# Binary cross-entropy over 8192 x 8192: three prediction slots and one 8-bit target slot in place of two slots each

## The chip, the cores and the metric

The kernel runs on one core of a Trainium2 chip. The metric is the device time of one execution in microseconds; the median of several runs is given. The work of this kernel is done by four kinds of unit: VectorE (DVE in the profile), ScalarE (ACT), GpSimd (POOL), which here only issues transfers, and the core's 16 DMA engines, which move data between HBM and SBUF. SyncE (SP) issues a few transfers too.

## The reference

```python
def setup_inputs():
    return {
        "pred": np.random.uniform(0.01, 0.99, (8192, 8192)).astype(np.float32),
        "target": np.random.randint(0, 2, (8192, 8192)).astype(np.float32),
    }

def reference(pred, target):
    eps = 1e-7
    pred = np.clip(pred, eps, 1 - eps)
    return -(target * np.log(pred) + (1 - target) * np.log(1 - pred))
```

Both inputs and the output are 8192 x 8192 in float32, 268.4 MB each. A target is 0 or 1. The kernel uses that: with p the clipped prediction and t the target, p + t - 1 is p where t is 1 and p - 1 where t is 0, so the natural logarithm of its absolute value, negated, is the result in both cases.

## The kernel before, in words

The matrices are read as flat arrays and cut into chunks. A chunk of width w is 128 partitions of w contiguous elements; the whole array is 524,288 columns of this kind. The function `plan` sets the widths and places: two chunks of 7680 columns, then 32 of 15360, two of 7680 and one of 1696; a side piece of 32 partitions x 1408 elements holds the remainder. SBUF has a ring of two slots of 15360 columns (60 KiB a partition) for predictions in float32 and one of the same columns for targets in bf16, with a small place for the last chunk. Targets are converted on the way in: the DMA reads float32 and writes bf16. The results overwrite the predictions in place and are stored from there.

Each chunk has five passes, most in two halves of 7680 columns:

- clip, L92, on DVE;
- merge, L95, on DVE (`scalar_tensor_tensor`: t - 1 + p);
- absolute value, L98, and logarithm, L99, on ACT;
- negate, L102, on DVE.

The order is written out by hand (`tc.manual_schedule()`): each engine does its instructions in the order of the program and waits at each for what it needs. Almost all transfers are issued by POOL into one queue, and the DMA engines serve that queue in order. In the main loop a chunk k is clipped and merged half by half, then negated half by half; then POOL gets the store of k (L78), the load of the targets of k+2 (L73) and the load of the predictions of k+2 (L74). With two slots, the last of these has to wait until the store of k has landed, since it writes into the same slot; POOL waits there with everything behind it. The first prediction chunk, the side piece and the last three stores go through SP's queue.

Of the kernel before, what the change touches and what calls it, by code (L numbers as in the profile page):

```python
# [1 line left out]

# [4 lines left out]

EPS = 1e-7

BIG = 15 * 1024  # L10
HALF = BIG // 2
SIDE = 1408


def plan(total):

    n, last = divmod(total, BIG)
    assert n > 4 and 0 < last <= 2048
    spots = [(HALF, 0), (HALF, HALF)]
    spots += [(BIG, k % 2 * BIG) for k in range(1, n - 1)]  # L20
    end = (n - 1) % 2 * BIG
    return spots + [(HALF, end), (HALF, end + HALF), (last - SIDE // 4, 2 * BIG)]

@with_exitstack
def kernel(
    ctx: ExitStack,
    tc: tile.TileContext,
    pred: bass.AP,  # L30
    target: bass.AP,
    out: bass.AP,
):
    nc = tc.nc
    fp32 = mybir.dt.float32
    bf16 = mybir.dt.bfloat16
    Alu = mybir.AluOpType
    Act = mybir.ActivationFunctionType
    P = nc.NUM_PARTITIONS

    R, C = pred.shape
    spots = plan(R * C // P)
    n = len(spots)
    widths = [w for w, _ in spots]
    turn = n // 2
    cut = R * C - sum(widths[:turn]) * P
    starts = [cut + sum(widths[:k]) * P for k in range(turn)]
    starts += [sum(widths[turn:k]) * P for k in range(turn, n)]

    def chunk(ap, k):  # L50
        flat = ap.rearrange("r c -> (r c)")
        return flat[starts[k] : starts[k] + widths[k] * P].rearrange("(p w) -> p w", p=P)

    pool = ctx.enter_context(tc.tile_pool(name="rings", bufs=1))
    ring = [P, 2 * BIG + widths[-1]]
    ring_p = pool.tile(ring, fp32, name="ring_p", tag="ring_p")
    ring_t = pool.tile(ring, bf16, name="ring_t", tag="ring_t")
    warm = pool.tile([1, 8], fp32, name="warm", tag="warm")
    side_p = pool.tile([32, SIDE], fp32, name="side_p", tag="side_p")
    side_t = pool.tile([32, SIDE], fp32, name="side_t", tag="side_t")  # L60

    def side(ap, j):
        flat = ap.rearrange("r c -> (r c)")
        return flat[cut - 32 * SIDE : cut].rearrange("(p w) -> p w", p=32)[j:32:4]

    def spot(ring, k, part=(0, 1)):
        w, c = spots[k]
        i, m = part
        return ring[:, c + i * w // m : c + (i + 1) * w // m]

    def load(k):
        queue = nc.sync if k == 0 else nc.gpsimd
        nc.gpsimd.dma_start(out=spot(ring_t, k), in_=chunk(target, k))  # L73
        queue.dma_start(out=spot(ring_p, k), in_=chunk(pred, k))  # L74

    def store(k):
        queue = nc.sync if k >= n - 3 else nc.gpsimd
        queue.dma_start(out=chunk(out, k), in_=spot(ring_p, k))  # L78

    def load_side():  # L80
        nc.vector.memset(side_p[:, 0:2], 0.5)  # L81
        nc.vector.memset(side_t[:, 0:2], 0.0)  # L82
        for j in range(4):
            nc.sync.dma_start(out=side_t[j:32:4, :], in_=side(target, j))
            nc.sync.dma_start(out=side_p[j:32:4, :], in_=side(pred, j))

    def store_side():
        for j in range(4):
            nc.sync.dma_start(out=side(out, j), in_=side_p[j:32:4, :])

    def front_of(p, t):
        nc.vector.tensor_scalar(  # L92
            out=p, in0=p, scalar1=EPS, scalar2=1 - EPS, op0=Alu.max, op1=Alu.min
        )
        nc.vector.scalar_tensor_tensor(  # L95
            out=p, in0=t, scalar=1.0, in1=p, op0=Alu.subtract, op1=Alu.add
        )
        nc.scalar.activation(out=p, in_=p, func=Act.Abs)  # L98
        nc.scalar.activation(out=p, in_=p, func=Act.Ln)  # L99

    def back_of(p):
        nc.vector.tensor_scalar(out=p, in0=p, scalar1=-1.0, scalar2=None, op0=Alu.mult)  # L102

    def front(k, *part):
        front_of(spot(ring_p, k, *part), spot(ring_t, k, *part))

    def back(k, *part):
        back_of(spot(ring_p, k, *part))

    with tc.manual_schedule():  # L110
        nc.vector.memset(warm, 1.0)  # L111
        for k in range(3):
            load(k)
        nc.scalar.activation(out=warm, in_=warm, func=Act.Ln)  # L114
        front(0)
        front(1)
        back(0)
        store(0)
        back(1)
        store(1)  # L120
        load(3)
        for k in range(2, n - 4):
            front(k, (0, 2))
            front(k, (1, 2))
            back(k, (0, 2))
            back(k, (1, 2))
            store(k)
            if k == n - 6:
                load_side()
            if k == n - 5:  # L130
                front_of(side_p, side_t)
            for j in range(k + 2, n if k == n - 5 else k + 3):
                load(j)
        z, a, b, c = range(n - 4, n)
        front(z, (0, 2))
        back_of(side_p)
        store_side()
        front(z, (1, 2))
        back(z, (0, 2))
        front(a)  # L140
        back(z, (1, 2))
        store(z)
        front(b, (0, 2))
        front(b, (1, 2))
        back(a)
        store(a)
        front(c)
        back(b)
        store(b)
        back(c)  # L150
        store(c)


# [1 line left out]
_INS = ['pred', 'target']  # L155
_OUTS = [((8192, 8192), 'float32')]


# [23 lines left out]
```

## Time and profile before

| quantity | value |
|---|---|
| time, median of 3 runs | 1865.92 us (1865.59 to 1866.86) |
| the profiled execution: its span | 1864.3 us |
| DVE busy | 1124.7 us (60%) |
| ACT busy | 902.1 us (48%) |
| POOL busy | 57.6 us (3%) |
| DMA, moved as counted in SBUF | 671.22 MB, mean 360 GB/s |
| HBM read and written | 536.87 MB and 268.44 MB, 432 GB/s |

The profiled execution has no timing of its own beside its span; the span runs from the first to the last instruction, and the median of the timed runs is 1.6 us longer. Lines of the timeline read: start in us, length in us, engine, line of the kernel, operation, output<-input, shapes, and in brackets the idle time of the engine just before and what ended it. Lines of the stretches read: from:to, length, busy time of DVE, ACT and POOL with the number of instructions, granted clock, mean busy share of the 16 DMA engines, GB/s. A packet counts wholly in the stretch in which it starts, so that in very short stretches the share can be above 1. Behind the views lie the trace's packet records (start, length and size of each DMA packet); here a packet of a large transfer is one partition's row.

### The profile page before, as it was taken

How to read it: one execution, taken by the hardware profiler on the slowest of the kernel's cores; microseconds unless marked ns; L12 is line 12 of the kernel's file. 1: busy time of each engine (PE TensorE's matmuls, PEld its weight loads, DVE VectorE, ACT ScalarE, POOL GpSimd, SP SyncE). 2: the span in 40 equal slices, each digit the busy share in tenths (PEclk: the TensorE clock that was granted, in tenths of full speed). 3: DMA queues.
4: the chain of work that ended last, by engine and by line, in shares of the span. 5: the costliest groups of instructions: out<-in, count | busy, mean ns of one | idle time of the engine just before them, and what ended most of it. 6: DMA issues, size and time to landing. Idle time of an engine off the chain costs nothing.

```text
span 1864.3 us, 649 instructions
## 1 busy us (share of the span) xinstructions
DVE 1124.7 (60%) x215; ACT 902.1 (48%) x144; POOL 57.6 (3%) x111
## 2 busy tenths in 40 slices
DVE  4655766555676655557665555766555576655585
ACT  3355553335555333555533355553335555333665
POOL 0000000000000000000000000000000000000000
DMA  9999999999999999999999999999999999999999
GB/s 295 376 357 340 357 339 370 386 380 355 341 355 343 369 388 379 356 341 355 349 364 388 380 355 343 353 353 360 389 378 355 349 348 353 359 388 384 347 341 385
DMA packets 16180, 671.22 MB, mean 360 GB/s; under 512 B 1872, under 2 KB 1872, under 8 KB 2352
## 3 DMA queue, kind: packets, MB, share of 16 engines
q0 software_dynamic: 15408, 657.98, 98.4%
q1 hardware_dynamic: 768, 13.21, 1.7%
q14 instruction: 4, 0.03, 0.0%
HBM read 536.87 MB, written 268.44 MB: 432 GB/s over the span
## 4 chain that ended last, share of the span: by engine, by line
DMA 35%; issue 26%; ACT 22%; DVE 15%; POOL 1%; DVEq 0%; POOLq 0%; PEldq 0%
DMA ring_p<-in_pred_dram 32%; ACT ring_p L98 11%; ACT ring_p L99 11%; DVE ring_p L95 7%; DVE ring_p L92 4%; DVE ring_p L102 4%; DMA out_dram<-ring_p 3%; POOL ring_t L73 0%; POOL out_dram L78 0%; DVEq L177 0%; POOL ring_p L74 0%; POOLq L78 0%; POOLq L73 0%; DVEq L92 0%; PEldq L177 0%
## 5 line engine op out<-in xcount | busy, mean ns | idle before, releaser
L98 ACT ACTIVATE ring_p<-ring_p 128x7680 f32<-128x7680 f32 (+1 forms) x70 | 450.3, 6433 | 933.4 <-DVE ring_p L95 933.4
L95 DVE SCALAR_TENSOR_TENSOR ring_p<-ring_t,ring_p 128x7680 f32<-128x7680 bf16 (+1 forms) x70 | 556.9, 7955 | 2.4
L92 DVE TENSOR_SCALAR ring_p<-ring_p 128x7680 f32<-128x7680 f32 (+1 forms) x70 | 283.8, 4055 | 397.9 <-DMA ring_p<-in_pred_dram 397.9
L102 DVE TENSOR_SCALAR ring_p<-ring_p 128x7680 f32<-128x7680 f32 (+1 forms) x69 | 283.8, 4114 | 321.2 <-ACT ring_p L99 321.2
L99 ACT ACTIVATE ring_p<-ring_p 128x7680 f32<-128x7680 f32 (+1 forms) x70 | 450.8, 6440 | 2.2
L74 POOL DMA_DIRECT2D ring_p<-in_pred_dram x36 | 19.3, 536 | 909.5 <-DMA out_dram<-ring_p 909.5
L78 POOL DMA_DIRECT2D out_dram<-ring_p x34 | 18.3, 539 | 852.0 <-DVE ring_p L102 827.7
L73 POOL DMA_DIRECT2D ring_t<-in_target_dram x37 | 20.3, 550 | 0.8 <-PEq L177 0.8
L98 ACT ACTIVATE side_p<-side_p 32x1408 f32<-32x1408 f32 x1 | 1.4, 1375 | 6.7 <-DVE side_p L95 6.7
L114 ACT ACT_TABLE_LOAD x1 | 1.3, 1283 | 0.7 <-PEq L166 0.7
L95 DVE SCALAR_TENSOR_TENSOR side_p<-side_t,side_p 32x1408 f32<-32x1408 f32 x1 | 1.6, 1611 | 0.0
L99 ACT ACTIVATE side_p<-side_p 32x1408 f32<-32x1408 f32 x1 | 1.4, 1375 | 0.0
L92 DVE TENSOR_SCALAR side_p<-side_p 32x1408 f32<-32x1408 f32 x1 | 0.9, 874 | 0.0
L102 DVE TENSOR_SCALAR side_p<-side_p 32x1408 f32<-32x1408 f32 x1 | 0.9, 873 | 0.0
L111 DVE MEMSET warm<- 1x8 f32 x1 | 0.1, 65 | 0.8 <-PEq L166 0.8
L114 ACT ACTIVATE warm<-warm 1x8 f32<-1x8 f32 x1 | 0.2, 208 | 0.0
L166 POOL MEMSET const-float32-0.0<- 128x1 f32 x1 | 0.1, 98 | 0.2 <-issue 0.2
L166 POOL MEMSET const-bfloat16-1.0<- 128x1 bf16 x1 | 0.1, 101 | 0.0
L166 POOL MEMSET const-uint8-127<- 128x1 uint8 x1 | 0.1, 99 | 0.0
L166 POOL MEMSET const-float32-1.0<- 128x1 f32 x1 | 0.1, 98 | 0.0
L81 DVE MEMSET side_p<- 32x2 f32 x1 | 0.1, 60 | 0.0
L82 DVE MEMSET side_t<- 32x2 f32 x1 | 0.1, 60 | 0.0
## 6 DMA issues: line engine op xcount, KB each, us to landing
ring_p<-in_pred_dram POOLq DMA_DIRECT2D x32, 7680.0 KB, 35.9
out_dram<-ring_p POOLq DMA_DIRECT2D x32, 7680.0 KB, 29.2
ring_t<-in_target_dram POOLq DMA_DIRECT2D x32, 3840.0 KB, 46.8
ring_p<-in_pred_dram POOLq DMA_DIRECT2D x3, 3840.0 KB, 35.7
ring_t<-in_target_dram POOLq DMA_DIRECT2D x4, 1920.0 KB, 28.2
out_dram<-ring_p POOLq DMA_DIRECT2D x2, 3840.0 KB, 28.1
out_dram<-ring_p SPq DMA_DIRECT2D x2, 3840.0 KB
ring_p<-in_pred_dram SPq DMA_DIRECT2D x1, 3840.0 KB
```

Of the source, the lines that this page charges most:

```text
L73: nc.gpsimd.dma_start(out=spot(ring_t, k), in_=chunk(target, k))
L74: queue.dma_start(out=spot(ring_p, k), in_=chunk(pred, k))
L78: queue.dma_start(out=chunk(out, k), in_=spot(ring_p, k))
L81: nc.vector.memset(side_p[:, 0:2], 0.5)
L82: nc.vector.memset(side_t[:, 0:2], 0.0)
L92: nc.vector.tensor_scalar(out=p, in0=p, scalar1=EPS, scalar2=1 - EPS, op0=Alu.max, op1=Alu.min)
L95: nc.vector.scalar_tensor_tensor(out=p, in0=t, scalar=1.0, in1=p, op0=Alu.subtract, op1=Alu.add)
L98: nc.scalar.activation(out=p, in_=p, func=Act.Abs)
L99: nc.scalar.activation(out=p, in_=p, func=Act.Ln)
L102: nc.vector.tensor_scalar(out=p, in0=p, scalar1=-1.0, scalar2=None, op0=Alu.mult)
L114: nc.scalar.activation(out=warm, in_=warm, func=Act.Ln)
L166: nc = _bacc.Bacc("TRN2", target_bir_lowering=False, num_devices=1)
```

## The change

Predictions get three slots of 15360 columns (60 KiB a partition each), targets one slot of 15360 columns in 8-bit integers (15 KiB a partition); the DMA converts from float32 to `uint8`. The widths are now 8704, 33 times 15360, and 8704 (35 chunks, numbered 0 to 34); the side piece and its small passes go. All chunks are worked in two halves.

The order changes too. The clips of chunk k+1 stand between the merges of k and the negates of k: clip first half of k+1, negate first half of k, clip second half of k+1, negate second half of k. The loads on POOL's queue are, for each chunk, target k+1 (after the merges of k, which free the single target slot), store k, and predictions k+2. The first prediction chunk is issued by ACT. Near the end, the last target chunk is loaded in two halves with the store of chunk 32 between them. The last store is cut: 7680 columns by POOL, and the last 1024 columns by SP as 108, 12 and 8 rows.

```diff
-BIG = 15 * 1024
-HALF = BIG // 2
-SIDE = 1408
...
+WIDE = 15360
+SIDE = 8704
+SLOTS = 3
+PARTS = 2
+REST = 1024
+ROWS = (108, 12, 8)
...
+    ring_p = pool.tile([P, SLOTS * WIDE], fp32, name="ring_p", tag="ring_p")
+    ring_t = pool.tile([P, WIDE], uint8, name="ring_t", tag="ring_t")
...
-    def load(k):
-        queue = nc.sync if k == 0 else nc.gpsimd
-        nc.gpsimd.dma_start(out=spot(ring_t, k), in_=chunk(target, k))
-        queue.dma_start(out=spot(ring_p, k), in_=chunk(pred, k))
+    def load_p(k):
+        queue = nc.scalar if k == 0 else nc.gpsimd
+        queue.dma_start(out=p_of(k), in_=chunk(pred, k))
+
+    def load_t(k, *cols):
+        cols = cols or (0, widths[k])
+        nc.gpsimd.dma_start(out=t_of(k, *cols), in_=chunk(target, k)[:, cols[0] : cols[1]])
...
-        queue = nc.sync if k >= n - 3 else nc.gpsimd
-        queue.dma_start(out=chunk(out, k), in_=spot(ring_p, k))
+        nc.gpsimd.dma_start(out=chunk(out, k), in_=p_of(k))
...
+    def store_last():
+        w = SIDE - REST
+        nc.gpsimd.dma_start(out=chunk(out, last)[:, :w], in_=p_of(last, 0, w))
+        r = 0
+        for rows in ROWS:
+            nc.sync.dma_start(
+                out=chunk(out, last)[r : r + rows, w:], in_=p_of(last, w)[r : r + rows, :]
+            )
+            r += rows
...
-        for k in range(2, n - 4):
-            front(k, (0, 2))
-            front(k, (1, 2))
-            back(k, (0, 2))
-            back(k, (1, 2))
-            store(k)
...
+        load_p(0)
+        load_t(0)
+        load_p(1)
+        nc.vector.memset(warm, 1.0)
+        nc.scalar.activation(out=warm, in_=warm, func=Act.Ln)
+        for i in range(PARTS):
+            clip(0, i)
+        for k in range(n):
+            for i in range(PARTS):
+                merge(k, i)
+            if k < last - 1:
+                load_t(k + 1)
+            elif k == last - 1:
+                load_t(last, 0, SIDE // PARTS)
+                store(last - 2)
+                load_t(last, SIDE // PARTS, SIDE)
+            for i in range(PARTS):
+                if k < last:
+                    clip(k + 1, i)
+                negate(k, i)
+            if k < last - 2:
+                store(k)
+            if k < last - 1:
+                load_p(k + 2)
+        store(last - 1)
+        store_last()
```

In the changed kernel clip is L85, merge L91, absolute value and logarithm L94 and L95, negate L99; the prediction load is L63, the target load L67, a store L70, and the last store L74 and L77.

## The prediction

> **What bounds the kernel now.** First the page: its span, its engines, its queues, and who waits for whom.
>
> ```profile
> span 1864.3 us, 649 instructions
> DVE 1124.7 (60%) x215; ACT 902.1 (48%) x144; POOL 57.6 (3%) x111
> DMA  9999999999999999999999999999999999999999
> q0 software_dynamic: 15408, 657.98, 98.4%
> HBM read 536.87 MB, written 268.44 MB: 432 GB/s over the span
> ```
>
> No engine is near full; the 16 DMA engines are, in every slice. Next the busy time in one long stretch, which leaves out 2.5 us at the head and 7.3 at the end (columns: stretch, its length, DVE, ACT, POOL, PE clock, DMA share, GB/s):
>
> ```profile
> 2.50:1857.00 1854.50, 1124.64 (x214) 900.61 (x142) 56.17 (x105) 1.00 1.00 361
> ```
>
> The share is 1.00, so the queue never runs dry there. A faster kernel would have to move the same 805 MB of HBM bytes in less, and only some 10 us of the span lie outside this stretch. Third, the pace, from the chain that ended last and then the timeline of one chunk (start, length, engine, line):
>
> ```profile
> 696.95 35.91 DMA ring_p<-in_pred_dram
> 805.64 35.93 DMA ring_p<-in_pred_dram
> ```
>
> ```profile
> 717.35 4.16 DVE L102 TENSOR_SCALAR ring_p<-ring_p 128x7680 f32<-128x7680 f32 x1 [8.97 <-ACT ring_p L99]
> 721.81 0.54 POOL L78 DMA_DIRECT2D out_dram<-ring_p  x1 [24.33 <-DVE ring_p L102]
> 722.33 0.55 POOL L73 DMA_DIRECT2D ring_t<-in_target_dram  x1
> 732.89 4.16 DVE L92 TENSOR_SCALAR ring_p<-ring_p 128x7680 f32<-128x7680 f32 x1 [11.38 <-DMA ring_p<-in_pred_dram]
> 737.08 8.16 DVE L95 SCALAR_TENSOR_TENSOR ring_p<-ring_t,ring_p 128x7680 f32<-128x7680 bf16 x1
> 745.16 4.15 DVE L92 TENSOR_SCALAR ring_p<-ring_p 128x7680 f32<-128x7680 f32 x1
> 745.28 6.60 ACT L98 ACTIVATE ring_p<-ring_p 128x7680 f32<-128x7680 f32 x1 [27.96 <-DVE ring_p L95]
> 751.28 0.54 POOL L74 DMA_DIRECT2D ring_p<-in_pred_dram  x1 [28.40 <-DMA out_dram<-ring_p]
> ```
>
> Two chunks take 108.69 us, one 54.345. It holds three transfers of 15360 columns, so 18.12 each. The middle one, the store, runs from the predictions' landing (732.89) to the release of the next load (751.28); the packet records give 18.11 for a target, 18.11 for a store and 18.12 for predictions, though the target writes half the bytes into SBUF. Thus the four-byte HBM side sets the time, and writing the targets as one byte takes nothing off. The store was issued at 721.81, 11 us before its turn: that lead keeps the engines fed.
>
> **The change part by part.** *8-bit targets.* Transfers: no gain by the row above (records: 2281 ns a target row written as bf16, 2267 ns a prediction row written as four bytes). A loss is hidden as long as a target transfer stays under the 18.3 us found below. The merge (L95) takes 8.16 us for 7680 columns of bf16 and 1.61 us for 1408 of f32, nearly one rate per column for two and four bytes; I take the same for one byte. Below, its lead is over 14 us a chunk, so only the two ends feel it.
>
> *One target slot, and a new order.* A chunk's transfers now stand on POOL's queue as target k+1, store k, predictions k+2. Target k+1 waits for both merges of k: issued some 17 us after target k landed, while store k-1 and predictions k+1 (36.2 us) are still moving. Lead 18 us, cost 0. Predictions k+2 need store k-1 landed, two transfers earlier: the 909.5 us that POOL sat before L74 go, but they were covered, so they bring nothing. Store k is what is late next. It waits for the second negate of k, and DVE's order now puts this behind both clips of k+1, interleaved. The first clip waits for predictions k+1. So from the moment these land, with only target k+1 left in the queue (18.11 us), the following must pass before the store's first packet:
>
> - last packet to the clip's start: 0.37 (records; the clip at 732.89 follows the last packet by that much);
> - four independent passes, clip, negate, clip, negate: 4.16 each, of which 0.08 overlaps the next (737.08 + 8.16 against 745.16), so 16.40;
> - DVE's end to POOL's issue: 0.30 (717.35 + 4.16 to 721.81);
> - issue to first packet on an idle engine. The trace has one such place, near the end, the store issued at 1819.64:
>
> ```profile
> 1819.64 0.54 POOL L78 DMA_DIRECT2D out_dram<-ring_p  x1 [32.73 <-DVE ring_p L102]
> ```
>
> ```profile
> 1820.40:1820.60 0.20, 0.00 (x0) 0.20 (x1) 0.00 (x0) 1.00 0.67 220
> 1820.60:1820.80 0.20, 0.00 (x0) 0.20 (x1) 0.00 (x0) 1.00 0.91 288
> 1820.80:1821.00 0.20, 0.00 (x0) 0.20 (x1) 0.00 (x0) 1.00 4.27 1774
> ```
>
> A packet is counted where it starts: some engines idle until 1820.80, then the store's 60 KiB rows begin (records: 1820.83). That is 1.20 us. Bounds: 0.54 (the issue alone) and 4.5 (the very first issue, 1.23 to 5.7).
>
> Sum 18.27, plus 0.05 because a restarted row took 2312 ns for 2267 and 0.05 (estimate; four engines restarted within 0.03) because 16 engines don't restart together: 18.37 against 18.11, a hole of 0.25 us. As a loop: 18.37 + store 18.11 + predictions 18.12 = 54.60 for 54.345. What matters is that the target isn't in this loop: even a target transfer of no length would leave 54.60. Holes come before stores 1 to 31: 31 x 0.25 = +7.9 us. Bounds by the two rows: 0 (no hole from 0.95 us down, so at 0.54) and 31 x 3.55 = 110 (4.5 us each time). The 4.5 was the first issue of all and the 1.20 one in full run, so I stay near the latter; the range takes in half as much again, 1.8 us or 27.
>
> The Trainium skill ("DMA: Bandwidth & Descriptors", section "Anatomy of one DMA — SWDGE (gpsimd) path") gives a fixed cost near 2.0 us for each such DMA, mostly completion. The rows above give 0.37 + 1.20 = 1.57 for what the loop sees of it. By the page the hole would be 0.43 larger, 13 us over 31 chunks; I go by the rows.
>
> *Engines in step.* In steady state the 16 engines now restart together each chunk. Early on single engines lose time at stores: the clips at 187.77, 242.55, 297.19, 351.57 and 406.83 are 54.78, 54.64, 54.38 and 55.26 apart, 1.7 us over pace. Before, such a loss stays on one engine; now each chunk waits for whichever slipped. Bounds 0 and 4, I take +2.
>
> *Head.* Predictions 0 go out on ACT's queue ahead of its table load (0.7 us in), as on SP's before (0.74). The queue holds 8704 + 8704 + 15360 columns, 38.7 us of work, to about 41. Target 0 has landed near 24 (2 x 10.3, after a first packet at 1.75 and some rows slow to start), the two merges take 4.6 each and end before 35, so target 1 is in time; store 0 comes 14.8 us after predictions 1 land (its negates are narrower), within target 1's 18.1. Cost 0. The memsets and the side piece (8 loads, 4 stores on SP, five small passes) go; their bytes lie in the chunks now.
>
> *End.* Count from the landing of target 33. Merges end at 8.1 and 16.2; ACT (two passes of 6.6 a half) is done at 21.4 and 34.6; the last negate at 38.8; store 33's first packet at 40.3. The engines meanwhile: predictions 34 (8704 columns, 10.27) to 9.9; half of target 34, ready at 9.6, to 15.0; store 32 to 33.1; the other half to 38.3. Idle 2.0 us. Store 33 runs to 58.4. Merges of 34 start at 38.8 behind the negate (4.6 a half), end at 48.0; ACT (3.75 a pass) ends at 58.5, the negate at 60.9, the first packet is at 62.4. Idle 4.0. Together 6.0. Against it: the end of before is ragged,
>
> ```profile
> 1860.00:1861.00 1.00, 0.00 (x0) 0.00 (x0) 0.00 (x0) 1.00 0.65 271
> 1861.00:1862.00 1.00, 0.00 (x0) 0.00 (x0) 0.00 (x0) 1.00 0.17 68
> 1862.00:1863.00 1.00, 0.00 (x0) 0.00 (x0) 0.00 (x0) 1.00 0.05 20
> ```
>
> 0.35 + 0.83 + 0.95 = 2.1 us, and 0.3 at 1820; engines that restart together save this 2.4. The last 1024 columns (512 KiB) as 108, 12 and 8 rows on SP: 1.2 us if spread evenly, up to 2.4 on half of the engines; I take 1.6, +0.4. End: 6.0 - 2.4 + 0.4 = +4.0 (bounds 2 and 6.4).
>
> Sum: 7.9 + 2 + 4 = +13.9 on the span, 1878.2. The median of the runs (1865.92) is 1.6 above this span, so 1879.8: 1880.
>
> **The rivals.** *The lead holds (not slower).* Where the store's first packet follows its issue by 0.95 us or less, the chain fits under the target's 18.11 and there is no hole; only the end is left: 1864.3 + 4 + 1.6 = 1869.9, between 1866 and 1872.5. For: the place at 1820 is a single one, and the margin is 0.25 us in 18. Against: the other links, 17.07 us, are seen many times over.
>
> *The restart costs more.* All 16 engines idle, and the measured place had most of them busy. At 2.0 instead of 1.57 for start and landing together (the size of the skill's figure), 1893; span 1890 to 1905. For: the very first issue took 4.5. Against: that one was cold.
>
> *The 8-bit write is dear.* If a target row took over 2.29 us, the target would set the pace: each 0.1 us more is 0.8 a chunk, 27 us in all. A merge of double length would cost some 25 at the two ends, nothing between. For: no one-byte row exists here. Against: halving the bytes changed 14 ns. 1890 to 1960.
>
> *Faster.* Needs the loop under 54.345 and the end without its two waits; the reserve is 5 us at most (span outside the full stretch, less head and landing): 1861. A gain from lighter targets alone is excluded by the loop.
>
> **How the numbers follow.** A difference up to 0.2% (3.7 us) is what a measurement here can't tell from none: 1862.2 to 1869.7. Forecast 0.52 (1872.5 to 1890), lead holds 0.18 (0.11 of it within 0.2%), dear restart 0.18, dear 8-bit 0.09, faster 0.03. Slower: 0.52 + 0.07 + 0.18 + 0.09 = 0.86; same 0.11; faster 0.03. From 1867 to 1896 what is left out is 0.03 of faster, 0.03 of the low cases, 0.08 of the restart and 0.06 of the 8-bit.
>
> **What would show it.** Right: clips of L85 54.6 us apart after the first 400 us; in that loop POOL's stores (L70) waiting for DVE (L99), issued about 17.1 us after the first clip's start; DMA share under 1.00 just before each store; no POOL wait of note at L63; two holes of 2 and 4 us in the last 60 us. Wrong: clips 54.35 apart (the lead holds), the store's packets over 1.5 us behind its issue, or target transfers longer than 18.3.

## The result, and the profile after

The changed kernel takes 1917.24 us (median; 1916.84 to 1917.39), the kernel before 1865.83 in the same comparison: 1.0272 times as long, 95% interval 1.0258 to 1.0286. The direction was as forecast; 1880 us and the range up to 1896 were too low. The profiled execution has a span of 1915.1 us, 50.8 more than before.

The page after, its span, engines, DMA slices, HBM bytes, and the time from issue to landing of the large transfers:

```profile
span 1915.1 us, 651 instructions
DVE 1113.2 (58%) x211; ACT 899.8 (47%) x142; POOL 57.6 (3%) x109
DMA  9999999999999999999999999999999999999997
HBM read 536.87 MB, written 268.44 MB: 421 GB/s over the span
...
ring_p<-in_pred_dram POOLq DMA_DIRECT2D x33, 7680.0 KB, 38.5
out_dram<-ring_p POOLq DMA_DIRECT2D x33, 7680.0 KB, 20.9
```

The same stretch as was read before, still with a mean DMA share of 1.00:

```profile
2.50:1857.00 1854.50, 1088.39 (x203) 870.06 (x135) 55.13 (x101) 1.00 1.00 315
```

The share is rounded: by the packet records an engine is idle for 11.6 us of this stretch on average, against 0.3 before. So some 11 of the 50 us that were lost are idle time; for most of the rest the engines are busy for longer with the same bytes. That is the first thing the forecast, which looked for a hole, did not have. The timeline of one chunk:

```profile
703.14 4.16 DVE L85 TENSOR_SCALAR ring_p<-ring_p 128x7680 f32<-128x7680 f32 x1 [21.46 <-DMA ring_p<-in_pred_dram]
707.22 4.15 DVE L99 TENSOR_SCALAR ring_p<-ring_p 128x7680 f32<-128x7680 f32 x1
711.29 4.15 DVE L85 TENSOR_SCALAR ring_p<-ring_p 128x7680 f32<-128x7680 f32 x1
715.36 4.15 DVE L99 TENSOR_SCALAR ring_p<-ring_p 128x7680 f32<-128x7680 f32 x1
719.81 0.54 POOL L70 DMA_DIRECT2D out_dram<-ring_p  x1 [37.30 <-DVE ring_p L99]
720.34 0.53 POOL L63 DMA_DIRECT2D ring_p<-in_pred_dram  x1
721.31 16.23 DVE L91 SCALAR_TENSOR_TENSOR ring_p<-ring_t,ring_p 128x7680 f32<-128x7680 uint8 x2 [1.80 <-DMA ring_t<-in_target_dram]
737.83 0.53 POOL L67 DMA_DIRECT2D ring_t<-in_target_dram  x1 [16.97 <-DVE ring_p L91]
758.86 4.16 DVE L85 TENSOR_SCALAR ring_p<-ring_p 128x7680 f32<-128x7680 f32 x1 [21.32 <-DMA ring_p<-in_pred_dram]
```

From clip to clip it is 55.72 us, 1.375 more than the 54.345 of before; times 31, 42.6 of the 50.8. The order of events is the one that was forecast: the clip waits for predictions, the store for the last negate, 16.67 us behind the clip. But the store then takes 20.9 us from issue to landing, where 1.1 to its first packet, 18.1 for its rows and 0.4 to landing would do. The packet records say where: each engine carries eight rows of a transfer, and the last row of the store is long. Mean length of the rows in us (over those engines whose packets can be told apart with certainty, 7 at least; the two long last rows over all 16), with the spread between the first and the last engine at the transfer's start and end:

```
kernel, transfer                     spread     row 1  2     3     4     5     6     7     8
before, predictions ahead of store 0 1.2  1.8   2.28  2.27  2.27  2.27  2.27  2.27  2.27  3.38
before, predictions in the middle    4.3  4.3   2.28  2.27  2.27  2.27  2.27  2.27  2.27  2.27
after, target                        0.6  0.6   2.28  2.28  2.28  2.28  2.28  2.28  2.28  2.28
after, store (at 720.9)              0.1  0.5   2.37  2.27  2.27  2.27  2.27  2.27  2.27  3.10
after, predictions behind it         0.6  0.4   2.33  2.27  2.27  2.27  2.27  2.27  2.27  2.27
```

The store's first packets come 1.1 us behind its issue, within 0.15 us of each other, and 0.02 to 0.15 us after the last engine ended the target: the hole is next to nothing on that engine, and up to 0.7 us on the others. What it does is to set all 16 engines in step, and the last row, ahead of the change from storing to loading, then costs 0.8 us more on average, over 1.1 on the slowest engine. The kernel before has such long rows on all engines once, ahead of its first store, when its engines were still within 2 us of each other; but that is a change from loading to storing. Later they are 4.3 us apart and the row is 2.27.

### The profile page after: what moved, and what is told of

Its sections match the earlier page's. It is cut to its first block, busy times and chain, and to the rows that moved or that the text cites. A ratio compares the mean times of both kernels' runs of the same rounds, so it can differ in the third digit from the quotient of the medians.

```text
span 1915.1 us, 651 instructions
## 1 busy us (share of the span) xinstructions
DVE 1113.2 (58%) x211; ACT 899.8 (47%) x142; POOL 57.6 (3%) x109
## 4 chain that ended last, share of the span: by engine, by line
DMA 67%; issue 30%; DVE 1%; POOL 0%; POOLq 0%; DVEq 0%; PEldq 0%
DMA ring_t<-in_target_dram 67%; DVE ring_p L91 1%; POOL ring_t L67 0%; POOL out_dram L70 0%; POOLq L153 0%; POOLq L67 0%; POOLq L70 0%; DVEq L91 0%; PEldq L153 0%; POOLq L74 0%
## 5 line engine op out<-in xcount | busy, mean ns | idle before, releaser
L94 ACT ACTIVATE ring_p<-ring_p 128x7680 f32<-128x7680 f32 (+1 forms) x70 | 450.5, 6436 | 991.1 <-DVE ring_p L91 991.1
L85 DVE TENSOR_SCALAR ring_p<-ring_p 128x7680 f32<-128x7680 f32 (+1 forms) x70 | 283.9, 4057 | 701.9 <-DMA ring_p<-in_pred_dram 701.9
L91 DVE SCALAR_TENSOR_TENSOR ring_p<-ring_t,ring_p 128x7680 f32<-128x7680 uint8 (+1 forms) x70 | 554.1, 7956 | 63.1 <-DMA ring_t<-in_target_dram 63.1
L95 ACT ACTIVATE ring_p<-ring_p 128x7680 f32<-128x7680 f32 (+1 forms) x70 | 451.1, 6444 | 2.2
L99 DVE TENSOR_SCALAR ring_p<-ring_p 128x7680 f32<-128x7680 f32 (+1 forms) x70 | 283.8, 4054 | 17.8 <-ACT ring_p L95 17.8
L70 POOL DMA_DIRECT2D out_dram<-ring_p x34 | 18.3, 538 | 1183.5 <-DVE ring_p L99 1183.5
L67 POOL DMA_DIRECT2D ring_t<-in_target_dram x36 | 20.8, 579 | 631.9 <-DVE ring_p L91 631.1
L63 POOL DMA_DIRECT2D ring_p<-in_pred_dram x34 | 18.0, 530 | 2.6 <-DMA out_dram<-ring_p 2.6
L74 POOL DMA_DIRECT2D out_dram<-ring_p x1 | 0.5, 538 | 21.8 <-DVE ring_p L99 21.8
## 6 DMA issues: line engine op xcount, KB each, us to landing
out_dram<-ring_p POOLq DMA_DIRECT2D x33, 7680.0 KB, 20.9
```

What stands on the lines that cost most here:

```text
L63: queue.dma_start(out=p_of(k), in_=chunk(pred, k))
L67: nc.gpsimd.dma_start(out=t_of(k, *cols), in_=chunk(target, k)[:, cols[0] : cols[1]])
L70: nc.gpsimd.dma_start(out=chunk(out, k), in_=p_of(k))
L74: nc.gpsimd.dma_start(out=chunk(out, last)[:, :w], in_=p_of(last, 0, w))
L85: nc.vector.tensor_scalar(out=p, in0=p, scalar1=EPS, scalar2=1 - EPS, op0=Alu.max, op1=Alu.min)
L91: nc.vector.scalar_tensor_tensor(out=p, in0=t, scalar=1.0, in1=p, op0=Alu.subtract, op1=Alu.add)
```

## The experiments

The theories: A, in step: the hole lines the engines up, and lined up they all pay at the change of direction. B: a store directly followed by a prediction load is slow whatever the phase (B2: only a prediction load, not a target load). C: POOL's issue and the end of the merge fall beside the store's last row. D: 8-bit conversion is dear. F: a transfer issued into an empty queue delays the one issued right behind it. Where a time stands without an interval, the kernel was run once.

**Negates ahead of the clips.**

```diff
-            for i in range(PARTS):
-                if k < last:
-                    clip(k + 1, i)
-                negate(k, i)
+            for i in range(PARTS):
+                negate(k, i)
+            for i in range(PARTS):
+                if k < last:
+                    clip(k + 1, i)
```

> DVE does both negates of chunk k before the clips of k+1, so the store of k is issued before the predictions of k+1 land and the queue has no hole; the store still stands directly ahead of a prediction load. Theory A (the hole lets all 16 engines restart in step, and in step the change from store to prediction load stretches the store's last row, 1.1 us a chunk): hole and stretch both go, clips 54.35 us apart, about 1873 us. Theory B (a store directly followed by a prediction load is slow whatever the engines' phase): only the hole and the slow first row go, some 0.35 us x 31 = 11 us, about 1906 us. Theory C (the stretch comes from POOL's issue of the next target and the end of DVE's merge, which fall beside the store's last row): unchanged by this edit, as B.

Measured 1882.96 us (1.0090 times before, 1.0075 to 1.0105). Its timeline:

```profile
694.00 8.23 DVE L85 TENSOR_SCALAR ring_p<-ring_p 128x7680 f32<-128x7680 f32 x2
694.38 3.89 POOL L70 DMA_DIRECT2D out_dram<-ring_p  x1 [21.99 <-DVE ring_p L99]
698.27 4.09 POOL L63 DMA_DIRECT2D ring_p<-in_pred_dram  x1
...
748.38 8.23 DVE L85 TENSOR_SCALAR ring_p<-ring_p 128x7680 f32<-128x7680 f32 x2
```

The chunk is 54.38 us, the pace of before, though a store still stands ahead of a prediction load and the next target's issue still falls beside the store's last rows. In its records the engines end 4.0 us apart in the middle and the store's last row is 2.27 us. Against B and C. The total is 10 us over what A gave: the middle is as A said, the end is longer than I had worked out: ahead of the last store no packet runs for 6.5 us, by the records.

**Predictions ahead of the store in the queue.**

```diff
+            if k < last - 1:
+                load_p(k + 2)
             for i in range(PARTS):
                 if k < last:
                     clip(k + 1, i)
                 negate(k, i)
             if k < last - 2:
                 store(k)
-            if k < last - 1:
-                load_p(k + 2)
```

> POOL issues the predictions of k+2 ahead of the store of k, so the queue is target, predictions, store, and the store is never waited for. Theory A: no hole, engines keep their spread, about 1868 to 1872 us. Theory B: the same, since no store stands ahead of a prediction load. Theory C: POOL's issue of the target still comes some 17 us after the target before landed, now beside the last row of a prediction load, which would be stretched instead: about 1900 us.

1880.15 us (1.0076, 1.0061 to 1.0091). Again nearly the pace of before in the middle (18.11 to 18.12 us from the end of most transfers to that of the next). Single engines still lose some tenths, early on up to 1.3 us, at the change from predictions to store; 17% of the last rows ahead of a store are over 2.5 us, and this drives the engines 6.6 us apart; the slowest sets the end. Of the 8 to 12 us above the forecast 3.0 are a stretch without any packet before the last store.

**A later store.**

```diff
             if k < last - 2:
+                negate(k, 1)
+                negate(k, 1)
                 store(k)
```

> Two more negates of the second half (8.2 us, values unchanged) before each store 0 to 31, so the hole before a store grows by about 8.2 us. A and B: the store's last row stays as slow as in the changed kernel, every chunk grows by just the 8.2 us: clips 63.9 us apart, some 2170 us. C: POOL's issue and the merge's end now fall beside the store's fourth row, so the last row is 2.27 us again and the chunk grows by some 1.1 us less: clips 62.8 apart, some 2135 us.

2179.27 us. The last row stays: 3.11 us, rows 2 to 7 at 2.27, and the store's landing is the same 20.9 as in the changed kernel. The hole grew by 8 us and the stretch did not change, so it goes with the restart and not with the hole's length. On C the run says less than I had expected: the merge had to wait for DVE too, and the target's issue came 16.1 us behind the store's, beside row 7 and not row 4.

```profile
out_dram<-ring_p POOLq DMA_DIRECT2D x33, 7680.0 KB, 20.9
```

**The kernel before with 8-bit targets.**

```diff
-    bf16 = mybir.dt.bfloat16
+    uint8 = mybir.dt.uint8
...
-    ring_t = pool.tile(ring, bf16, name="ring_t", tag="ring_t")
+    ring_t = pool.tile(ring, uint8, name="ring_t", tag="ring_t")
```

> The kernel before with its target ring in 8-bit integers in place of bf16, nothing else. Theory D (converting to 8 bits is dear for the DMA or for the merge): more than 1875 us. A, B and C: no difference, 1864 to 1868 us.

1866.55 us, 1.0001 times before (0.9991 to 1.0011); target rows are 2281 ns as with bf16, and the merge costs the same. The group of that line:

```profile
L95 DVE SCALAR_TENSOR_TENSOR ring_p<-ring_t,ring_p 128x7680 f32<-128x7680 uint8 (+1 forms) x70 | 556.9, 7955 | 2.4
```

D is out: 8 bits neither cost nor gain.

**The kernel before with a late store.**

```diff
             back(k, (1, 2))
+            for _ in range(4):
+                back(k, (1, 2))
             store(k)
```

> The kernel before, with the second half of each chunk negated four more times (16.4 us of DVE, values unchanged), so that here too the queue is empty when the store is issued and all engines restart together; behind the store stands a target load. DVE's chain sets the pace, about 59.4 us a chunk, some 2030 us in all. Theory A (engines in step stretch the last row ahead of any change from storing to loading): a store takes 1.0 + 18.1 + 1.2, about 20.3 us from issue to landing, its last row 3.1 us. Theory B2 (it takes a plain prediction load behind the store): 19.2 us, last row 2.27.

2050.09 us. Here a target load stands behind the store, and the targets are bf16 in two slots; still the store's last row is 2.98 to 3.11 us on average, with the engines 0.13 us apart at its start. So the stretch is no property of the new slots, of 8 bits or of the prediction load (against B2): a restart in step brings it to the old kernel. POOL issues nothing between 744.66 and 764.72 in its timeline, while the store of that chunk starts at 744.6 and ends its last rows from 763.4 to 764.1, and the merge beside it goes on to 764.5: C is out. The landing time expected can't be read off, as the issue itself took 3.89 us beside a clip.

**Shorter last chunks.** Predictions ahead of the store as above, and

```diff
-SIDE = 8704
+TAIL = [13312, 7168, 2048]
...
-    widths = [SIDE] + [WIDE] * (n - 2) + [SIDE]
+    rest = total - sum(TAIL)
+    widths = [rest % WIDE] + [WIDE] * (rest // WIDE) + TAIL
...
```

which gives 10240, 32 x 15360, 13312, 7168 and 2048 columns, with one order for all chunks and no special end.

> Predictions ahead of the store on POOL's queue as in the earlier run (1880 us), and the widths 10240, 32 x 15360, 13312, 7168, 2048, with all chunks in the same order and each store whole on POOL. If the 14 us that run kept over the kernel before lie in its end, where the last chunks' stores wait for ACT, this one comes out at 1864 to 1868 us; if they lie elsewhere, at 1878 or more.

1875.32 us (1.0047, 1.0033 to 1.0061): between the two. Five of the 14 us lay in the long end. The engines drift 7.3 us apart.

**Uneven pieces of the store.**

```diff
+    def store_uneven(k):
+        w = WIDE - REST
+        nc.gpsimd.dma_start(out=chunk(out, k)[:, :w], in_=p_of(k, 0, w))
+        r = 0
+        for rows in (12, 8, 4) * 4 + (12, 4) * 2:
+            nc.sync.dma_start(
+                out=chunk(out, k)[r : r + rows, w:], in_=p_of(k, w)[r : r + rows, :]
+            )
+            r += rows
...
-            if k < last - 2:
+            if 0 < k < last - 2:
+                store_uneven(k)
...
```

> The changed kernel; the last 1024 columns of each store 1 to 31 go out through SP in pieces of 12, 8 and 4 rows, issued with the store, so that some engines get up to 16 short rows more and others none, and they reach the change to the prediction load some 2.5 us apart, in four groups. The hole before the store stays. The engine with most work is 1.3 us later than the mean. Theory A (in step): the store's last row falls back toward 2.3 us and the clips are 54.6 + 1.3 = 55.9 us apart. Theory F (whatever the phase, a transfer issued into an empty queue delays the one behind it): last rows stay 3.1 us, clips 57.1 apart.

1973.83 us, clips 57.2 to 57.9 us apart. Inconclusive: the small pieces were still going out when the prediction load had begun, so both ends of the change were mixed. Of a store's 128 large rows 6.5 were over 2.5 us, against 16 in the changed kernel.

**The store in two.**

```diff
-        nc.gpsimd.dma_start(out=chunk(out, k), in_=p_of(k))
+        for r in (0, P // 2):
+            nc.gpsimd.dma_start(
+                out=chunk(out, k)[r : r + P // 2, :], in_=p_of(k)[r : r + P // 2, :]
+            )
```

> The changed kernel; each store 0 to 32 is issued as two transfers of 64 partitions one behind the other, both after the second negate. Each engine gets four rows of the first and four of the second. Theory A: only the last row of the second half, ahead of the prediction load, is stretched (3.1 us), time as the changed kernel, about 1917 us. Theory F: the delay moves to the seam between the halves, the fourth row, or shows at both.

2594.68 us: a miss for every theory. A transfer of 64 partitions ran at half the rate, 4.79 us a row for 2.27 on all 16 engines, so the seam tells nothing; the rate is taken up below.

**Extra loads, uneven and even.**

```diff
+            if 0 < k < last - 2:
+                nc.vector.memset(p_of(k + 2, 0, 1)[: EXTRA[0], :], 0.5)
+                for j, rows in enumerate(EXTRA):
+                    cols = slice(j * WIDE // 3, (j + 1) * WIDE // 3)
+                    nc.sync.dma_start(
+                        out=p_of(k + 2, cols.start, cols.stop)[:rows, :],
+                        in_=chunk(pred, k + 2)[:rows, cols],
+                    )
```

`EXTRA` is (4, 8, 12) in the uneven kernel and (16, 16, 16) in its control.

> The changed kernel; with each store 1 to 31, SP loads 5120 columns of predictions k+2 ahead of time into their slot for 4, for 8 and for 12 partitions (rows of 20 KiB, about 0.76 us each; the full load then writes the same values again). Engines get 3, 2, 1 or no extra rows beside the store, so they reach the change to the prediction load up to 2.3 us apart; the full load is issued some 6 us behind the store and still 12 us ahead of its turn. Theory A (in step): the store's last row falls from 3.1 to at most 2.5 us on average; the engines with three extra rows set the pace, 54.6 + 2.3 = 56.9 us a chunk. Theory F (an empty queue delays the follower whatever the phase): last rows stay 3.1 us, 58.0 a chunk.

> The control to the uneven one: three extra loads of 16 partitions each, one row for each of the 16 engines, so the engines stay in step and everything else is as there. Theory A: last rows stay near 3.1 us, 55.7 + 2.3 = 58.0 us a chunk. If the later issue of the full load, and not the engines' phase, were what mended the uneven one, the last rows here would be 2.3 us too, and the chunk 56.9.

2074.97 and 2100.26 us. In the uneven one the last row fell to 2.30 us on average, as A said. But the control did not keep the engines in step: loads beside the store's first rows stretched many of those to 2.5 to 2.9 us by different amounts, and the engines ended 3 to 4 us apart in it too, with last rows of 2.27. Both agree with A, and neither alone tells it from F, since the full load was issued later in both. Chunks grew to 61 to 62 us, more than either theory gave.

**A later load, and nothing else.**

```diff
-            for i in range(PARTS):
-                merge(k, i)
+            merge(k, 0)
+            if 1 <= k < last - 1:
+                nc.vector.memset(p_of(k + 1, 0, 1), 0.5)
+                load_p(k + 1)
+            merge(k, 1)
...
-            if k < last - 1:
+            if k == last - 2:
                 load_p(k + 2)
```

> The changed kernel, with the predictions of k+2 issued only after the first half of the merge of k+1 (a one-column memset of their slot makes POOL wait): some 10 us behind the store instead of 0.5, into a queue that is busy with the store, and still 8 us ahead of their turn. No DMA work is added and the hole before the store stays, so the engines restart in step as before. Theory A (in step): nothing changes, last rows of stores 3.1 us, clips 55.7 us apart, about 1917 us. Theory F (what matters is that the load is issued right behind a store that went into an empty queue): last rows 2.27 us, clips 54.6 apart, about 1881 us.

1921.61 us. Its timeline:

```profile
705.78 4.16 DVE L85 TENSOR_SCALAR ring_p<-ring_p 128x7680 f32<-128x7680 f32 x1 [21.51 <-DMA ring_p<-in_pred_dram]
...
722.44 0.54 POOL L70 DMA_DIRECT2D out_dram<-ring_p  x1 [37.35 <-DVE ring_p L99]
...
732.32 0.53 POOL L63 DMA_DIRECT2D ring_p<-in_pred_dram  x1 [9.34 <-DVE ring_p L112]
...
761.61 4.16 DVE L85 TENSOR_SCALAR ring_p<-ring_p 128x7680 f32<-128x7680 f32 x1 [21.52 <-DMA ring_p<-in_pred_dram]
```

The load is issued 9.9 us behind the store and the chunk is still 55.8 us, the last row 3.11. Against F. It also makes more of the extra loads: a later load alone leaves the stretch, so what took it away there was the engines' distance at the store's end, or the extra loads themselves.

**Negates first, with shorter last chunks.**

> Both negates ahead of the clips, as in the run at 1883 us, with the widths 10752... (first chunk what is left over), 32 x 15360, 13312, 9216, 4096, 1024 and one order for all chunks. The run at 1883 kept the kernel before's pace in the middle and lost some 15 us at its end. With the shorter last chunks 1866 to 1872 us; at 1878 or more the loss lies elsewhere.

The edit is that of the first experiment with the widths 5120, 32 x 15360, 13312, 9216, 4096, 1024. 1881.92 us (1.0087, 1.0073 to 1.0101), a miss: the narrow first chunk opens a hole ahead of the store of chunk 1, and the end has holes of its own. (The expectation's 10752 was a slip; 5120 columns are left over.)

This run holds what no other does: two stores one after the other, both of 15360 columns, both ahead of a prediction load and both with the engines within 0.7 us of each other, the first behind a hole and the second not. The issues of the two, and the stretches ahead of the first store and within the second:

```profile
93.71 3.89 POOL L69 DMA_DIRECT2D out_dram<-ring_p  x1 [22.00 <-DVE ring_p L87]
140.50 3.89 POOL L69 DMA_DIRECT2D out_dram<-ring_p  x1 [21.99 <-DVE ring_p L87]
```

```profile
96.60:98.10 1.50, 1.50 (x2) 0.00 (x0) 1.50 (x2) 1.00 0.00 0
155.00:170.70 15.70, 15.39 (x2) 7.16 (x2) 0.00 (x0) 1.00 1.00 434
```

The rows in us, with the spread of the engines at the start and end, over all 16:

```
transfer                             spread     row 1  2     3     4     5     6     7     8
store 1, behind the hole (98.16)     0.2  0.6   2.31  2.28  2.33  2.27  2.27  2.27  2.27  3.08
target 3 (135.11)                    0.6  0.7   2.28  2.28  2.28  2.28  2.28  2.28  2.29  3.29
store 2, no hole ahead (154.26)      0.7  0.7   2.28  2.27  2.27  2.27  2.27  2.27  2.27  2.27
```

Store 2 was issued 14 us before target 3 ended. Its engines are 0.7 us apart, close enough to pay over 1 us at the last row of target 3, and yet the change to the load behind the store costs nothing. So A, as worded above, does not hold: engines in step do not pay at every change. Behind a hole they pay at the end of the store, otherwise at the end of the load ahead of it. Store 1 differs from store 2 in two ways, its start on an empty queue and engines only 0.1 us apart when its last rows began; this run does not tell which of them counts.

**The last store through SP.**

```diff
-        nc.gpsimd.dma_start(out=chunk(out, last)[:, :w], in_=p_of(last, 0, w))
+        nc.sync.dma_start(out=chunk(out, last)[:, :w], in_=p_of(last, 0, w))
```

> The changed kernel with the 7680-column piece of the last store issued by SP in place of POOL, ahead of the three small pieces. If ending on a POOL-issued store is what holds the span open for 5.4 us after the last packet, the span ends some 1.3 us after it and the time falls by about 4 us, to 1913. If not, 1917.

1913.28 us (1.0251, 1.0235 to 1.0267), 4.0 us less. The last stretches of the changed kernel, and below them those of this one:

```profile
1905.00:1909.00 4.00, 0.00 (x0) 0.00 (x0) 0.00 (x0) 1.00 0.89 384
1909.00:1912.00 3.00, 0.00 (x0) 0.00 (x0) 0.00 (x0) 1.00 0.00 0
1912.00:1915.10 3.10, 0.00 (x0) 0.00 (x0) 0.00 (x0) 1.00 0.00 0
```

```profile
1909.00:1910.00 1.00, 0.00 (x0) 0.00 (x0) 0.00 (x0) 1.00 0.71 262
1910.00:1911.80 1.80, 0.00 (x0) 0.00 (x0) 0.00 (x0) 1.00 0.07 25
```

No packet starts after 1909 in the changed kernel (the last one ends at 1909.7 by the records), yet its span goes on to 1915.1, 5.4 us. With the store on SP it ends 1.3 us behind the last packet, as in the kernel before.

**Both mended.** The same for the last two stores of the kernel with shorter last chunks:

```diff
-        nc.gpsimd.dma_start(out=chunk(out, k), in_=p_of(k))
+        queue = nc.sync if k >= last - 1 else nc.gpsimd
+        queue.dma_start(out=chunk(out, k), in_=p_of(k))
```

> The run at 1875 us (predictions ahead of the store, last chunks 13312, 7168, 2048) with the stores of the last two chunks issued by SP. By the same reasoning about 4 to 5 us less, 1870 to 1871, still above the kernel before; if the ending on POOL's queue costs nothing, 1875.

1871.28 us (1.0028, 1.0018 to 1.0038). The best form of the new slots that was run, and still slower than before. No kernel here beats the old one.

## Why the prediction was wrong

*Bound, and the 8-bit targets:* right. The transfers set the time, and one-byte targets change nothing (1.0001).

*The loop:* right in its form, wrong in one term. The forecast had the store's first packet 18.00 us behind the clip's start; it is 17.8. Predictions and landing took 18.5 together, as forecast. The store was put at 18.11 and took 19.4. Together 55.72 for 54.60. The hole itself, on the last engine, is 0.02 to 0.15 us, where the forecast had 0.25. (The sign given for it, stores issued 17.1 us behind the clip, took in the landing, which comes before the clip; by the prediction's own terms it is 16.70, and 16.67 was measured.)

*"Engines in step":* the step that failed. It said that the engines now restart together and that what the kernel before shows of slips would cost 2 us, between 0 and 4; and the loop had the store at its undisturbed 18.11. In its place the runs showed a last row of 3.1 us in each store that starts behind a hole, about 1.3 us a chunk. It counted single slips from the clips' distances in an execution where the engines were soon 4 us apart. The one place of that trace where they were close together, ahead of the first store, has last rows of 3.38 us for 2.27, and was not priced: 1.1 us for each of 31 changes is 34, and the sum would have been 1912. Even that would have been partly luck: that place, like the single slips, is a change from loading to storing, while the changed kernel pays at the change from storing to loading, which costs nothing in that trace.

*Rivals:* the dear restart was the nearest in size, but not in kind: the start took 1.1 us, less than the 1.20 assumed, and its 1893 would still have been 24 us short.

*Head:* right, no hole there. *End:* right in part. The last store's first packet came 62.4 us behind the last packet of target 33, as forecast, after 2.8 us without a packet (4.0 were forecast). The wait of 2.0 us ahead of store 33 did not come: the first half of the last target took 7.9 us for the 5.1 worked out and filled it. The 4.1 us more after the last packet of a POOL-issued store were not foreseen. 42.6 for the loop and 4.1 for that leave 4.1 of the 50.8 for all the rest.

What the runs show of the cause: five kernels whose stores start behind a hole (the changed one, the two later stores, the later load, the last store through SP) have the stretch in each chunk, and store 1 of the last run with negates first has it too. Kernels without the hole lose it at the stores' end, and have their long rows ahead of the stores instead, fewer and fewer as the engines drift apart. Rows over 2.5 us, by the packet records:

| kernel | ahead of a store | ahead of the load behind a store |
|---|---|---|
| before | 35 | 0 |
| negates first | 69 | 2 |
| predictions first | 88 | 0 |
| changed | 16, all at its store 0, which has no hole | 495 of 512 |

So the hole is what brings the stretch to the store's end, and since it lines the engines up anew in each chunk, the price never wears off. That the engines must also be in step is less sure: it rests on the two runs with extra loads, where the holes stayed, the engines were 3 to 6 us apart at the store's end and the last row was 2.27 to 2.31.

What stays open: why it is the last row, why a hole moves the price from the load ahead of a store to the store's own end (by the start on an empty queue, or by bringing the engines within 0.15 us; the extra loads, whose stores started on an empty queue with the engines 1.6 to 1.8 us apart, speak for the latter), and how close the engines must be at each kind of change.

## What to carry to other kernels

When the DMA engines are the bound, being busy is not the same as moving at full rate: look at the length of rows ahead of each change between loading and storing. Keep every store issued well before its turn, since a queue that runs dry even for 0.1 us lines the engines up and the price comes some 16 us later, at the other end of the transfer. And issue the very last store from SP rather than POOL, 4 us here.

## What the runs showed of the hardware

- POOL's issue of a transfer takes 0.54 us, but 3.89 and 4.09 us beside DVE's clips in float32 (the timeline of the first experiment), and 0.53 beside the merge. The Trainium skill ("SBUF — State Buffer", section "SBUF: two separate sides") says that GpSimd can't write the descriptors of a transfer while DVE runs an operation that takes both of its ports, and gives about 620 ns for a transfer alone against 3100 beside a DVE copy. The runs agree: the first of these issues ended 0.1 us behind the first clip, the second 0.1 us behind the second. It cost nothing here, as the target ahead of the store in the queue ran for 7 us more.
- A transfer of 64 partitions moved at half the rate of one of 128 (4.79 us for a 60 KiB row, 2.27 otherwise, with 16 engines busy in both). The Trainium skill ("SBUF — State Buffer", section "Door 1: The DMA port swizzle") says that the rate depends on how many of 16 ports the partitions reach, and that partitions 0 to 63, or 64 to 127, reach eight. The rows agree.
- The span ends 1.3 us after the last packet if SP issued it, 5.4 if POOL did.
- Left alone the engines drift 3 to 4 us apart within some 450 us, one by one, at changes from loading to storing; in the kernel before and the one with negates first they then keep about this distance, with predictions first they go on to 6.6.
